# Sample attention of a hybrid decoder layer: steps for a pair of batches, scores of 64 rows by 32 columns

## The chip, the core and the metric

The kernel runs on one core of a Trainium2 chip. The core has five engines that run their own instruction streams: TensorE (PE: matmuls, with PEld for the weight loads that go beside them), VectorE (DVE), ScalarE (ACT), GpSimd (POOL) and SyncE (SP), which here issues the transfers (DMA) between the main memory and the on-chip memory. TensorE writes its results into banks of PSUM, from which VectorE and ScalarE read. The metric is the device time of one launch in microseconds.

## What the kernel computes

One layer for a prompt of 512 positions and for a sample group of 8 batches with 8 new positions each. The same normalised input goes through one combined projection `w_in` (2048 rows), then through sparse attention with three branches and a gated linear recurrence (RG-LRU), both of which are projected and merged. The sample group's attention is the part that the change touches:

```
q, kv..., g_nsa, g_att, x_rnn, g_rnn, gm_att, gm_rnn = _project(x, norm_g, w_in, ...)   # 16 heads of 64, 4 key heads
k_c, v_c = _compress(past_cmp, w_cmp, gain)           # 2048 past positions -> 64 compressed ones
o_cmp, imp = _cmp_branch(q, k_c, v_c, q_pos)          # softmax over them; importance of 32 blocks
sel_idx = _select_blocks(imp, q_pos)                  # the best 15 of 32 blocks of 64 positions
s = einsum('btgrd,btgkd->btgrk', q, k[selected]) * SCALE;  o_sel = softmax(s) @ v[selected]
s = einsum('btgrd,bkgd->btgrk', q, k[window 512]) * SCALE; o_win = softmax(s) @ v[window]
o_att = g_cmp * o_cmp + g_sel * o_sel + g_win * o_win
```

A batch has 8 positions x 4 query heads = 32 query rows for each of the 4 key heads, against 2048 past keys (in four blocks of 512, the unselected masked by a bias) and 512 window keys, a fifth block.

## The kernel before

The projections are the frame of the program. The weights go through in "slots": a slot is 24 matmuls of 128x128 by 288 columns (eight slices of weights, each three times: high part by high part, high by low, low by high), of which `L1710` to `L1712` are the three lines. The weights of a unit arrive by one transfer (`raw`, L226), ScalarE makes their high part (`whi`, L233) and VectorE the low part (`wlo`, L239), every second slot. All other work is put between the slots, and the order in which the Python code emits it is the order on each engine.

In the slots of the RG-LRU's two projections (168 to 231, 64 slots; 734 to 1026 us of the profile), the code emits, ahead of the slot's 24 matmuls: the weight split's high part, then the functions that were put on that slot by `at(slot, f)` (parts of the RG-LRU chunk: `split`, `decay`, `scan`), then the sample attention's next step (`sample_work`), then the low part and the next load of weights, then the read-out of finished projection banks, and last the functions put "behind" (the gate products `gate(0)`, `gate(1)` at L1242). An RG-LRU chunk has 8 slots. A gate product uses one bank of "s" and one of "t".

`sample_steps` writes out by hand what is done in which step: `put(t, order, f, x)` puts a function into step t, and within a step the smaller order goes first. Batch b has its scores of block n2 at step 8 + 5b + n2, and there are 52 steps, one in nearly every slot, so several batches are under way at once. For a block: `k_load` (L995, four transfers of 128 KB for four pages, three steps ahead), `v_load` (L1005), `k_scores` (L915, through `s_scores`), `k_max` on VectorE (L1019; L1024 and L1025 for the window: mask, maximum, copy out of the bank), `s_exp` on ScalarE (L1030), two steps later four transposes (L1035) and their copy (L1039), and one step after that the products with V (L1049) into the batch's output bank "o". `c_norm`, `c_root`, `c_keys`, `x_scores`, `x_exp`, `x_prob`, `x_sum`, `x_select` make the compressed branch and the choice of blocks (L892 to L957), `x_new`, `x_turn_`, `x_turned`, `x_out` the new keys (L963 to L986), and `s_factors`, `s_total`, `s_sum` (L1075, L1076), `s_fin` (L1080) and `s_put` (L1085) the end of a batch.

The score products of a batch are four matmuls, one for each key head:

```
for h in range(4):
    T.matmul(dst[h * 32:h * 32 + 32], x.q[:, h], k(h // 2), start=True, stop=True)
```

Each takes 128 rows of keys (two key heads stand one above the other, 64 rows each) by 32 columns of queries, whose other 64 rows are zero (`q_batch`). The four go to four column groups of the array and write the four quarters of one bank. In single precision each matmul is two passes, so it has two records in the trace.

PSUM has two banks each of "g" (projection), "s" and "t", and one of "o" and one of "m" (small products).

Of the kernel before, what the change touches and what calls it, by code (L numbers as in the profile page):

```python
# [16 lines left out]
KEPT = 3  # L17
# [96 lines left out]
def nsa_rglru_step(ctx, tc, a, o):  # L114
# [259 lines left out]
    gR = ar.tile([128, 3, DB], F, name="gR")  # L374
# [15 lines left out]
    def evac(kind, h, b):  # L390
# [9 lines left out]
        if name == "gn":  # L400
# [5 lines left out]
            if h == 1:  # L406
                def sigmoids():
                    V.tensor_mul(t[:48], t[:48], rstd[:48])
                    A.activation(t[:48], t[:48], AF.Tanh, scale=0.5)
                    V.tensor_scalar(t[:48], t[:48], 0.5, 0.5, op0=OP.mult, op1=OP.add)  # L410
                at(NORM + 2, sigmoids)

                def gates():
                    m = bank("m")
                    for i in range(4):
                        T.transpose(m[:, i * 48:i * 48 + 48], t[:48, i * 128:i * 128 + 128], ident[:48, :48])
                    V.tensor_copy(gT.rearrange("p i c -> p (i c)"), m[:, :192])
                at(NORM + 4, gates)

                def rows():  # L420
                    S.dma_start(gs_d, t[:48, 512:576])
                    for br in range(3):
                        S.dma_start(gR[:, br, :], gs_d[br * 16:br * 16 + 16, :].rearrange("g (t b) -> (g t) b", b=8))
                at(NORM + 4, rows)
# [415 lines left out]
    def q_batch(x):  # L840

        x.q = pp["s"].tile([128, 4, 32], F, tag="qb", name="qb", bufs=3)
        G.memset(x.q, 0.0)
        for c in range(2):
            for gl in range(2):
                me = slice(gl * 64, gl * 64 + 64)
                V.tensor_copy(x.q[me, c * 2 + gl].rearrange("p (r t) -> p r t", t=8), zs[me, c, :, x.b:64:8])

# [4 lines left out]
    for b, x in enumerate(batches):  # L853
        x.b = b
        x.P, x.T, x.V, x.K, x.cr = {}, {}, {}, {}, {}
# [21 lines left out]
    def c_reduce(x, n):  # L877
        if n == 0:
            x.kvx = pp["x"].tile([128, 4, 80], F, tag="skvx", name="skvx", bufs=3)
# [5 lines left out]
    def c_fetch(x):  # L885
        if x.b >= KEPT:
            x.kvx = pp["x"].tile([128, 4, 80], F, tag="skvx", name="skvx", bufs=3)
            S.dma_start(x.kvx[:, :, 8:72], kc_d[x.b])

    def c_square(x):  # L890
        x.sq = pp["s"].tile([128, 2, 64], F, tag="ssq", name="ssq", bufs=2)
        A.activation(x.sq, x.kvx[:, 0:2, 8:72], AF.Square)  # L892
        for c, new in ((0, kn), (2, vn)):
            for br in range(2):
                G.tensor_copy(x.kvx[:, c:c + 2, br * 72:br * 72 + 8], new[:, :, br, x.b:64:8])

    def c_norm(x):
        sq = x.sq
        m = bank("m")
        T.matmul(m[:, :128], C("bones"), sq.rearrange("p c n -> p (c n)"), start=True, stop=True)  # L900
        x.m = m

    def c_root(x):
        sq, m = x.sq, held_bank("m", x.m)
        V.tensor_scalar(sq.rearrange("p c n -> p (c n)"), m[:, :128], 1.0 / HD, EPS, op0=OP.mult, op1=OP.add)
        A.activation(sq, sq, AF.Sqrt)

    def c_keys(x):
        V.reciprocal(x.sq, x.sq)
        V.scalar_tensor_tensor(x.kvx[:, 0:2, 8:72], x.kvx[:, 0:2, 8:72], P("gk0"), x.sq, OP.mult, OP.mult)  # L910

    def s_scores(dst, x, k):

        for h in range(4):
            T.matmul(dst[h * 32:h * 32 + 32], x.q[:, h], k(h // 2), start=True, stop=True)  # L915

    def x_scores(x):

        x.m = bank("m")
        s_scores(x.m[:, :80], x, lambda c: x.kvx[:, c, :])  # L920
# [4 lines left out]
    def x_exp(x):  # L925
        m = held_bank("m", x.m)
        x.e = pp["s"].tile([128, 80], F, tag="se", name="se", bufs=3)
        x.sm = pp["s"].tile([128, 32], F, tag="ssm", name="ssm", bufs=4)
        sm = x.sm
        V.tensor_reduce(sm[:, CN:CN + 1], m[:, 8:72], axis=AX.X, op=OP.max, negate=True)  # L930
        V.tensor_add(x.e[:, 0:8], m[:, 0:8], C("snew"))
        V.tensor_add(x.e[:, 72:80], m[:, 72:80], C("snew"))
        A.activation(x.e[:, 8:72], m[:, 8:72], AF.Exp, bias=sm[:, CN:CN + 1], accum_out=sm[:, CS:CS + 1])

    def x_prob(x):
        sm = x.sm
        V.tensor_scalar_max(sm[:, CS:CS + 1], sm[:, CS:CS + 1], TINY)
        V.reciprocal(sm[:, CS:CS + 1], sm[:, CS:CS + 1])
        V.tensor_scalar_mul(x.e[:, 8:72], x.e[:, 8:72], sm[:, CS:CS + 1])

    def x_sum(x):
        x.m = bank("m")
        T.matmul(x.m[:, :64], C("rsum"), x.e[:, 8:72], start=True, stop=True)

    def x_select(x):
        m = held_bank("m", x.m)
        imp = pp["s"].tile([128, 32], F, tag="imp", name="imp", bufs=2)
        v8 = pp["s"].tile([128, 2, 8], F, tag="v8", name="v8", bufs=2)
        V.tensor_reduce(imp, m[:, :64].rearrange("p (n two) -> p n two", two=2), axis=AX.X, op=OP.add)
        V.memset(imp[:, 0:32:31], -2.0)  # L950
        V.max(v8[:, 0], imp)
        V.match_replace(imp, v8[:, 0], imp, -2.0)
        V.max(v8[:, 1], imp)
        V.memset(v8[:, 1, 5:8], -2.0)
        V.match_replace(imp, v8[:, 1], imp, -2.0)
        x.bias = pp["s"].tile([128, 32], F, tag="sbias", name="sbias", bufs=2)
        V.tensor_scalar(x.bias, imp, -1.5, NEG, op0=OP.is_gt, op1=OP.mult)  # L957

    def x_new(x):

        sm, e = x.sm, x.e
        for n, at_ in ((4, 0), (6, 72)):
            V.tensor_reduce(sm[:, NM + n:NM + n + 1], e[:, at_:at_ + 8], axis=AX.X, op=OP.max, negate=True)  # L963
        for n, at_ in ((4, 0), (6, 72)):
            A.activation(e[:, at_:at_ + 8], e[:, at_:at_ + 8], AF.Exp, bias=sm[:, NM + n:NM + n + 1],
                         accum_out=sm[:, SUM + n:SUM + n + 1])

    def x_turn_(x):
        t = x.tx = bank("t")
        T.transpose(t[:80, 0:128], x.e, ident)  # L970
        for c in range(2):
            T.transpose(t[:80, 128 + c * 128:256 + c * 128], x.kvx[:, 2 + c, :], ident)

    def x_turned(x):

        t = held_bank("t", x.tx)
        x.pt = pp["s"].tile([128, 640], F, tag="vx", name="vx", bufs=2)
        for n in range(3):
            A.activation(x.pt[:80, n * 128:n * 128 + 128], t[:80, :128], AF.Copy, scale=C("xm")[:80, n:n + 1])
        A.activation(x.pt[:80, 384:], t[:80, 128:384], AF.Copy)  # L980

    def x_out(x):
        ob = held_bank("o", x.o)
        for n, part in enumerate((4, 6, 7)):
            for h in range(4):
                T.matmul(ob[h * 32:h * 32 + 32, part * 64:part * 64 + 64], x.pt[:80, n * 128 + h * 32:n * 128 + h * 32 + 32],  # L986
                         x.pt[:80, 384 + h * 64:448 + h * 64], start=True, stop=True)

    def k_load(x, n2):

        t = pp["s"].tile([128, 1024], F, tag="kr", name="kr", bufs=4)
        if n2 < 4:
            x.K[n2] = t.rearrange("p (k c n) -> p k c n", k=4, c=2)
            for k in range(4):
                S.dma_start(t[:, k * 256:k * 256 + 256],  # L995
                            a["selk"][ds(page(x.b, 4 * n2 + k, "k"), 1)].rearrange("o p c f -> p (o c f)"))
        else:
            x.K[n2] = t.rearrange("p (c k n) -> p k c n", k=4, c=2)
            S.dma_start(t, a["wink"][x.b].rearrange("p c n -> p (c n)"))

    def v_load(x, n2):
        t = x.V[n2] = pp["s"].tile([128, 4, 256], F, tag="vr", name="vr", bufs=4)
        if n2 < 4:
            for k in range(4):
                S.dma_start(t[:, k], a["selv"][ds(page(x.b, 4 * n2 + k, "v"), 1)].rearrange("o p f -> p (o f)"))  # L1005
        else:
            S.dma_start(t, a["winv"][x.b])

    def k_scores(x, n2):
        x.s = bank("s")  # L1010
        t = x.K.pop(n2)
        s_scores(x.s.rearrange("p (k n) -> p k n", k=4), x, lambda c: t[:, :, c])

    def k_max(x, n2):

        s, sm = held_bank("s", x.s), x.sm
        p = x.P[n2] = pp["s"].tile([128, 512], F, tag="p", name="sp", bufs=4)
        if n2 < 4:
            V.tensor_tensor_reduce(p.rearrange("p (n k) -> p n k", k=64), s.rearrange("p (n k) -> p n k", k=64),  # L1019
                                   x.bias[:, n2 * 8:n2 * 8 + 8, None].to_broadcast([128, 8, 64]), -1.0, 3.0e38,  # L1020
                                   OP.add, OP.min, sm[:, NM + n2:NM + n2 + 1])
        else:
            to = sm[:, NM + 5:NM + 6]
            V.tensor_tensor_reduce(p[:, :8], s[:, :8], C("wm"), -1.0, 3.0e38, OP.add, OP.min, sm[:, CN:CN + 1])  # L1024
            V.tensor_tensor_reduce(p[:, 8:], s[:, 8:], C("zero").to_broadcast([128, 504]), -1.0, sm[:, CN:CN + 1],  # L1025
                                   OP.add, OP.min, to)

    def s_exp(x, n2):
        p, n = x.P[n2], n2 + n2 // 4
        A.activation(p, p, AF.Exp, bias=x.sm[:, NM + n:NM + n + 1], scale=-1.0, accum_out=x.sm[:, SUM + n:SUM + n + 1])  # L1030

    def s_turn(x, n2):
        t = x.t = bank("t")
        for k in range(4):
# [778 lines left out]
```

## Time and profile before

| what | value |
|---|---|
| median of 3 runs | 1663.26 us (1661.42 to 1664.68) |
| the profiled execution's own time | 1661.96 us |
| its span in the trace | 1660.2 us, 34348 instructions |
| TensorE busy | 1620.8 us (98% of the span) |
| VectorE, ScalarE, GpSimd busy | 1133.5 us (68%), 788.2 us (47%), 300.7 us (18%) |
| the chain that ended last | PE 72%, DVE 13%, ACT 9%, DMA 3%, issue 3% |
| score products (L915) in the chain | 2% of the span |

Busy is the time during which an engine had at least one instruction under way. The chain is followed back from the last instruction, at each step to what released it. The span begins a little after the launch and so is shorter than the time.

### The profile page before, as it was taken

The numbers are of one execution on the slowest core, as the hardware profiler recorded it, in microseconds if no ns is written. First come the engines' busy times: TensorE is split into PE (matmuls) and PEld (weight loads), VectorE is DVE, ScalarE is ACT, GpSimd is POOL, SyncE is SP. The second block draws the span as 40 slices with busy tenths as digits, with TensorE's granted clock in tenths as the row PEclk, the third lists the DMA queues.
The fourth block names the chain that finished last, engine by engine and source line by source line (L and its number), as shares of the span: only waits on it lengthen the run. The fifth ranks groups of instructions, "written<-read, shape, count | busy, mean of one in ns | idle before, by whom it ended". The sixth has DMA issues, their size and how long they took to land.

```text
span 1660.2 us, 34348 instructions
## 1 busy us (share of the span) xinstructions
PE 1620.8 (98%) x13309; PEld 1552.1 (93%) x13309; DVE 1133.5 (68%) x2259; ACT 788.2 (47%) x1449; POOL 300.7 (18%) x367
## 2 busy tenths in 40 slices
PE   9989999999999999999999999999998999999999
PEld 8989989998998999997878879999998999999999
DVE  7768778867876886566666766766665443358775
ACT  6353554555355454467776766444443222233332
POOL 0014443543444254400000000000000111110000
PEclk9999999999999999999999999999999999999999
DMA  6186634533533444437667673732337454456442
GB/s 229 62 292 236 198 105 122 176 108 100 183 122 114 135 151 144 139 122 233 211 209 239 221 227 98 231 133 107 123 127 256 149 165 160 142 198 225 135 154 74
DMA packets 132486, 272.18 MB, mean 164 GB/s; under 512 B 20321, under 2 KB 60386, under 8 KB 132066
## 3 DMA queue, kind: packets, MB, share of 16 engines
q1 hardware_dynamic: 132322, 269.98, 49.5%
q8 instruction: 105, 1.72, 0.4%
q14 instruction: 59, 0.48, 0.1%
HBM read 235.16 MB, written 43.15 MB: 168 GB/s over the span
## 4 chain that ended last, share of the span: by engine, by line
PE 72%; DVE 13%; ACT 9%; DMA 3%; issue 3%; SPq 1%; POOL 0%; ACTq 0%; DVEq 0%; POOLq 0%
PE g L1710 15%; PE g L1712 15%; PE g L1711 15%; DVE wlo L239 2%; PE g L1373 2%; PE g L1372 2%; PE g L1371 2%; ACT whi L233 2%; PE g L1471 2%; PE g L1473 2%; PE g L1472 2%; PE s L915 2%; PE t L748 1%; DVE pt L752 1%; ACT p L733 1%
## 5 line engine op out<-in xcount | busy, mean ns | idle before, releaser
L1710 PE MATMUL g<-xh,whi 128*128 128x288 f32 x1920 | 577.8, 301 | 0.1
L1712 PE MATMUL g<-xh,wlo 128*128 128x288 f32 x1920 | 567.5, 296 | 1.6 <-DVE wlo L239 1.6
L1711 PE MATMUL g<-xl,whi 128*128 128x288 f32 x1920 | 567.2, 295 | 0.0
L1710 PEld LDWEIGHTS g<-xh,whi 128*128 128x128 f32 x1920 | 362.5, 189 | 24.3 <-issue 18.3
L1711 PEld LDWEIGHTS g<-xl,whi 128*128 128x128 f32 x1920 | 362.5, 189 | 1.3
L1712 PEld LDWEIGHTS g<-xh,wlo 128*128 128x128 f32 x1920 | 361.8, 188 | 2.0 <-DVE wlo L239 2.0
L239 DVE TENSOR_TENSOR wlo<-raw,whi 128x1024 fp32r<-128x1024 f32 x164 | 221.4, 1350 | 33.4 <-ACT whi L233 32.1
L875 POOL TENSOR_TENSOR cr<-cr,wcs 128x512 f32<-128x512 f32 x128 | 182.6, 1431 | 164.1 <-DMA cr<-in_cmp 149.0
L233 ACT ACTIVATE whi<-raw 128x1024 fp32r<-128x1024 f32 x164 | 172.4, 1051 | 33.3 <-PE g L1711 24.2
L733 ACT ACTIVATE p<-p,sm,rq 128x128 f32<-128x128 f32 (+3 forms) x128 | 82.8, 648 | 154.4 <-DVE sm L730 154.2
L752 DVE TENSOR_TENSOR pt<-t,pt 128x512 fp32r<-128x512 f32 x96 | 66.1, 689 | 64.3 <-ACT pt L751 63.1
L741 POOL TENSOR_SCALAR p<-p,sm 128x128 f32<-128x128 f32 (+3 forms) x128 | 68.0, 544 | 208.3 <-DVE sm L738 88.0
L576 POOL TENSOR_TENSOR ur<-ur,tgi 128x288 f32<-128x288 f32 x32 | 25.7, 804 | 410.5 <-DVE tgi L575 338.6
L881 DVE TENSOR_REDUCE skvx<-cr 128x16 f32<-128x512 f32 x128 | 86.7, 678 | 0.4
L1710 PE MATMUL g<-hrh,whi 128*128 128x288 f32 x256 | 76.7, 299 | 6.5 <-ACT gm L532 4.2
L751 ACT ACTIVATE pt<-t 128x512 fp32r<-128x512 f32 x96 | 56.5, 592 | 55.0 <-PE t L748 54.3
L582 ACT ACTIVATE mh<-ur 128x288 fp32r<-128x288 f32 x32 | 14.2, 445 | 143.1 <-POOL ur L576 143.1
L1712 PE MATMUL g<-hrh,wlo 128*128 128x288 f32 x256 | 76.0, 297 | 0.0
L1711 PE MATMUL g<-hrl,whi 128*128 128x288 f32 x256 | 76.0, 297 | 0.0
L1712 PE MATMUL g<-oah,wlo 128*128 128x288 f32 x256 | 75.4, 295 | 0.0
L1711 PE MATMUL g<-oal,whi 128*128 128x288 f32 x256 | 75.3, 294 | 0.0
L1710 PE MATMUL g<-oah,whi 128*128 128x288 f32 x256 | 75.3, 294 | 0.0
(435 smaller groups left out, 3673.6 us busy)
## 6 DMA issues: line engine op xcount, KB each, us to landing
raw<-in_w_in SPq DMA_DIRECT2D x124, 512.0 KB, 3.6
cr<-in_cmp SPq DMA_DIRECT2D x128, 256.0 KB, 3.6
kr<-in_selk SPq DMA_DIRECT2D x128, 128.0 KB, 3.2
vr<-in_selv SPq DMA_DIRECT2D x128, 128.0 KB, 3.7
a<-in_w_in SPq DMA_DIRECT2D x28, 512.0 KB, 4.2
tgi<-tg SPq DMA_DIRECT2D x32, 288.0 KB, 4.4
yr<-in_w_out SPq DMA_DIRECT2D x18, 512.0 KB, 5.3
raw<-in_w_rnn SPq DMA_DIRECT2D x16, 512.0 KB, 4.5
```

What stands on the lines that cost most here:

```text
L233: A.activation(hi, raw[k], AF.Copy)
L239: V.tensor_sub(lo, raw.pop(k), hi.bitcast(F))
L733: A.activation(p[:, :n], p[:, :n], AF.Exp, bias=sm[:, 1, r - r0:r - r0 + 1], scale=rq[:, i, r:r + 1], accum_out=sm[:, 2, r - r0:r - r0 + 1])
L741: G.tensor_scalar(p[:, :n], p[:, :n], sm[:, 3, r - r0:r - r0 + 1], 1.0, op0=OP.mult, op1=OP.mult)
L751: A.activation(hi, t, AF.Copy)
L752: V.tensor_sub(lo, t, hi.bitcast(F))
L875: G.tensor_tensor(v, v, wcs[:, :, None, :].to_broadcast([128, 4, 4, 32]), op=OP.mult)
L881: V.tensor_reduce(x.kvx[:, :, 8 + n * 4:12 + n * 4], v, axis=AX.X, op=OP.add)
L915: T.matmul(dst[h * 32:h * 32 + 32], x.q[:, h], k(h // 2), start=True, stop=True)
L1710: T.matmul(gb[:, :HF], wh[:, k, :], r_h[:, hs], start=kk == 0, stop=False)
L1711: T.matmul(gb[:, :HF], wh[:, k, :], r_l[:, hs], start=False, stop=False)
L1712: T.matmul(gb[:, :HF], wl[:, k, :], r_h[:, hs], start=False, stop=last and k == 7)
```

## The change

The unit of the steps becomes a pair of batches. All 128 partitions of a row of work now hold two batches and two of the four key heads: unit u = 0 has the key heads in the upper 64 rows, u = 1 those in the lower 64. Scores are made by eight matmuls for a pair, each of 64 rows by 32 columns: four column groups (two batches by two key heads) in each half of the rows. The halves write two different "s" banks, one for each unit. The queries need no zeros (`q_pair`). `k_max`, `s_exp`, the transposes, their copy and the V products have the same sizes and the same number as before, two per step, one for each unit. The output banks of the units are "o" and "m"; what used "m" before now uses "t". The smaller functions (`x_prob`, `x_select`, `x_new`, `s_factors`, `s_total`) do both units in one instruction where they can; `s_put` makes 16 copies per pair in place of 4. The gates' factors come through `gB` (12 small transfers) and a copy on GpSimd.

Pair n has its scores at steps 5 + 6n to 9 + 6n, the window's block first, and there are 32 steps. `sample_work` spreads the steps evenly over the same 64 slots, so a step comes in every second slot, the one that does not split weights. Keys are loaded one step ahead, transposes are made one step after the scores, V products two.

```diff
     def s_scores(dst, x, k):
-        for h in range(4):
-            T.matmul(dst[h * 32:h * 32 + 32], x.q[:, h], k(h // 2), start=True, stop=True)
+        for n in range(2):
+            for c in range(2):
+                j = (n * 2 + c) * 32
+                for u in UNITS:
+                    T.matmul(dst[u][j:j + 32], x.q[ROWS[u], n, c * 32:c * 32 + 32], k(n, c)[ROWS[u]], start=True, stop=True)
...
     def k_scores(x, n2):
-        x.s = bank("s")
+        x.s = [bank("s") for _ in UNITS]
         t = x.K.pop(n2)
...
     def s_sum(x):
+        for u in UNITS:
+            ob = held_bank("om"[u], x.o[u]).rearrange("p (n d) -> p n d", d=64)
+            t = pp["s"].tile([128, 512], F, tag="p", name="to", bufs=4).rearrange("p (n d) -> p n d", d=64)
+            V.tensor_mul(t, ob, x.sm[:, u, FAC:FAC + 8, None].to_broadcast([128, 8, 64]))
+            V.tensor_reduce(x.t2[:, u], t.rearrange("p n d -> p d n"), axis=AX.X, op=OP.add)
...
     def s_put(x):
+        for n, y in enumerate(x.b):
+            for pr in range(2):
+                for u in UNITS:
+                    for c in range(2):
+                        V.tensor_copy(o6[pr * 64:pr * 64 + 64, c, u, :, :, y.b], m[:, u, n, c, :, pr, :])
...
-        for x in batches:
-            s = 8 + 5 * x.b
...
+        for x in pairs:
+            s = 4 + 6 * x.n
+            put(s, 4, x_scores, x)
...
+            put(s + 2, 5, x_sum, x)
+            put(s + 2, 7, x_select, x)
+            for k, n2 in enumerate((4, 0, 1, 2, 3)):
+                t = s + 1 + k
+                put(t - 1, 0, k_load, x, n2)
+                put(t + 1, 0, v_load, x, n2)
+                put(t, 4, k_scores, x, n2)
+                put(t, 8, k_max, x, n2)
+                put(t, 9, s_exp, x, n2)
+                put(t + 1, 1, s_turn, x, n2)
+                put(t + 1, 1.5, s_turned, x, n2)
+                put(t + 2, 2, s_out, x, n2)
...
+            put(s + 8, 3, x_out, x)
+            put(s + 8, 7, s_sum, x)
+            put(s + 9, 5, s_fin, x)
+            put(s + 9, 7, s_put, x)
```

The order of the instructions at two places. On TensorE, a step of the sample attention between two slots' matmuls, before (L1035 transposes, L1049 V products, L915 scores into "s" and, the last row but one, of the compressed keys into "m"):

```order
L1710 MATMUL g<-xh,whi 128x288
L1711 MATMUL g<-xl,whi 128x288
L1712 MATMUL g<-xh,wlo 128x288
L1035 MATMUL t<-cst,sp 128x128 x4
L1049 MATMUL o<-vr,spt 32x64 x16
L915 MATMUL s<-kr,qb 32x512 x4
L915 MATMUL m<-skvx,qb 32x80 x4
L1710 MATMUL g<-xh,whi 128x288
```

And after, at a step with a gate product of the RG-LRU behind it (L1078 transposes, L1095 V products into the banks "o" and "m", L941 scores, L1296 the gate product):

```order
L1764 MATMUL g<-xh,whi 128x288
L1765 MATMUL g<-xl,whi 128x288
L1766 MATMUL g<-xh,wlo 128x288
L1078 MATMUL t<-cst,sp 128x128 x8
L1095 MATMUL o<-vr,spt 32x64 x16
L1095 MATMUL m<-vr,spt 32x64 x16
L941 MATMUL s<-kr,qb 32x512 x8
L1296 MATMUL s<-xb,bdh 128x288
L1296 MATMUL s<-xb,bdl 128x288
L1296 MATMUL t<-xb,bdh 128x288
```

The transposes and V products of two units now stand in one step, the eight score matmuls write both banks "s", and the gate product, which takes the next "s" bank, stands right behind them.

On VectorE, the end of a chunk's scan (L1261 to L1277) with the end of one batch behind it, before (L1075 and L1076 are `s_sum`, L1019 is `k_max`, L930 belongs to `x_exp`):

```order
L1261 SCALAR_TENSOR_TENSOR hh<-aa,ti 128x576
L1262 COPY hout<-hh 128x1
L1263 COPY hout<-hh 128x8
L1277 TENSOR_TENSOR rg<-rg,hh 128x64
L1075 TENSOR_TENSOR to<-o,ssm 128x512
L1076 TENSOR_REDUCE t_10723<-to 128x64
L1019 ISA sp,ssm<-s,sbias 128x512
L1019 ISA ssm 128x1
L930 TENSOR_REDUCE ssm<-m 128x1
```

And after, at step 12 (L1315 to L1331 the scan, L1124 and L1125 `s_sum`, L975 to L980 the start of `x_select`; the two `k_max`, L1060, come eight rows further on):

```order
L1315 SCALAR_TENSOR_TENSOR hh<-aa,ti 128x576
L1316 COPY hout<-hh 128x1
L1317 COPY hout<-hh 128x8
L1331 TENSOR_TENSOR rg<-rg,hh 128x64
L1124 TENSOR_TENSOR to<-o,ssm 128x512
L1125 TENSOR_REDUCE t_10583<-to 128x64
L1124 TENSOR_TENSOR to<-m,ssm 128x512
L1125 TENSOR_REDUCE t_10583<-to 128x64
L975 TENSOR_REDUCE imp<-t 128x64
L976 MEMSET imp 128x2x2
L978 MAX v_10591<-imp 128x8
L979 MATCH_REPLACE imp<-v_10591,imp 128x32
```

Behind the scan there are now two units' sums and a pair's selection of blocks ahead of `k_max`, where one batch's sum stood before.

## Rows read from the trace of the kernel before

**Rows 1.** The busy time by stretch, here the sum of three stretches that make up 740 to 1010 us: busy us of each engine in 270 us, and their means per stretch (a mean of the three, not a share).

```profile
sum 270.00, PE 261.56 PEld 220.35 DVE 185.28 ACT 195.19 POOL 16.35; mean PE 87.19 PEld 73.45 DVE 61.76 ACT 65.06 POOL 5.45
```

**Rows 2.** TensorE's groups of instructions between 727 and 1030 us. Columns: line, engine, operation, output and inputs, tile, shape, count, then busy us and mean ns of one, then the idle time just before them and what ended it.

```profile
L1710 PE MATMUL g<-xh,whi 128*128 128x288 f32 x473 | 143.4, 303 | 0.0
...
L915 PE MATMUL s<-kr,qb 128*32 128x512 f32 x320 | 42.6, 604 | 0.0
...
L900 PE MATMUL m<-ssq,cst 128*128 128x128 f32 x16 | 3.3, 287 | 3.0 <-ACT ssq L892 3.0
...
L970 PE MATMUL t<-cst,se 128*80 128x128 f32 x8 | 2.3, 285 | 2.8 <-ACT ti L1245 2.6 <-ACT spt L1039 0.2
L1080 PE MATMUL m<-cst,t 128*64 128x128 f32 x7 | 2.0, 283 | 2.7 <-ACT se L933 2.7
```

**Rows 3.** TensorE's timeline at a cluster with a score block. Columns: start us, us from the first start to the last end, engine, line, operation, tiles, shape, records.

```profile
876.97 0.60 PE L1035 MATMUL t<-cst,sp 128*128 128x128 f32 x4
877.41 0.33 PE L943 MATMUL m<-se,cst 128*128 128x64 f32 x2
877.67 0.65 PE L1049 MATMUL o<-vr,spt 128*32 128x64 f32 x32
878.14 1.04 PE L915 MATMUL s<-kr,qb 128*32 128x512 f32 x8
879.11 0.40 PE L1710 MATMUL g<-xh,whi 128*128 128x288 f32 x1
```

**Rows 4.** The same view at a cluster of the last steps, which has no score block.

```profile
1013.02 0.60 PE L1035 MATMUL t<-cst,sp 128*128 128x128 f32 x4
1013.55 0.65 PE L1049 MATMUL o<-vr,spt 128*32 128x64 f32 x32
1014.13 0.40 PE L1710 MATMUL g<-xh,whi 128*128 128x288 f32 x1
1014.37 0.29 PE L1711 MATMUL g<-xl,whi 128*128 128x288 f32 x1
1014.50 0.29 PE L1712 MATMUL g<-xh,wlo 128*128 128x288 f32 x1
```

**Rows 5.** The same view at the longest wait of this stretch (in brackets: idle us before, and what ended it).

```profile
777.75 0.60 PE L1035 MATMUL t<-cst,sp 128*128 128x128 f32 x4
780.89 0.49 PE L900 MATMUL m<-ssq,cst 128*128 128x128 f32 x2 [2.54 <-ACT ssq L892]
...
781.78 1.77 PE L915 MATMUL s<-kr,qb 128*32 128x512 f32 x8
```

**Rows 6.** The busy time by stretch, just after that wait: busy us and instructions of PE, PEld, DVE, ACT and POOL, the granted clock as a share of full speed, the DMA engines' share and GB/s.

```profile
782.00:785.00 3.00, 3.00 (x14) 1.52 (x7) 2.96 (x9) 1.20 (x3) 2.29 (x8) 0.50 0.81 268
```

**Rows 7.** VectorE's groups of instructions between 740 and 1010 us, columns as in Rows 2.

```profile
L1019 DVE CUSTOM_DVE_ANT_1 sp<-s,sbias 128x512 f32<-128x512 f32 x32 | 21.9, 685 | 15.9 <-PE s L915 15.9
...
L1261 DVE TENSOR_TENSOR_SCAN hh<-aa,ti 128x576 f32<-128x576 f32 x7 | 9.5, 1358 | 0.2
L1263 DVE COPY hout<-hh 128x8 f32<-128x8 f32 x7 | 9.3, 1326 | 0.0
...
L1076 DVE TENSOR_REDUCE t<-to 128x64 f32<-128x512 f32 x7 | 7.5, 1078 | 0.2
...
L1255 DVE TENSOR_TENSOR ti<-ti,tr 128x576 f32<-128x576 f32 x7 | 5.3, 754 | 0.3 <-ACT tr L1250 0.3
L1025 DVE CUSTOM_DVE_ANT_0 sp<-s,cst,ssm 128x504 f32<-128x504 f32 x7 | 5.2, 743 | 0.2
...
L1075 DVE TENSOR_TENSOR to<-o,ssm 128x512 f32<-128x512 f32 x7 | 4.8, 686 | 2.8 <-PE o L1049 2.8
...
L1019 DVE DVE_READ_ACCUMULATOR2_ANT ssm<- 128x1 f32 x32 | 2.6, 83 | 0.0
```

**Rows 8.** The busy time by stretch, from the first to the last instruction of one batch's selection (L949 to L957, ten instructions on VectorE), columns as in Rows 6.

```profile
877.78:879.42 1.64, 1.64 (x42) 0.80 (x42) 1.33 (x10) 1.53 (x3) 0.14 (x1) 1.00 0.87 264
```

**Rows 9.** ScalarE's groups of instructions between 740 and 1010 us, columns as in Rows 2.

```profile
L1030 ACT ACTIVATE sp<-sp,ssm 128x512 f32<-128x512 f32 x39 | 28.0, 719 | 39.4 <-DVE ssm L1019 27.4 <-DVE ssm L1025 11.9
L233 ACT ACTIVATE whi<-raw 128x1024 fp32r<-128x1024 f32 x25 | 26.2, 1050 | 0.8 <-PE g L1711 0.6
...
L1250 ACT ACT_TABLE_LOAD x7 | 9.0, 1283 | 0.1
...
L1030 ACT ACTIVATION_READ_ACCUMULATOR sp<-sp,ssm 128x1 f32 x39 | 7.3, 187 | 0.0
...
L1249 ACT ACTIVATE tr<-tr,lc 128x576 f32<-128x576 f32 x7 | 6.1, 870 | 0.2
L1245 ACT ACTIVATE ti<-s,lc 64x288 f32<-64x288 f32 x12 | 6.0, 498 | 0.1
...
L1248 ACT ACTIVATE aa<-tr,lc 128x576 f32<-128x576 f32 x6 | 5.1, 852 | 0.0
...
L1250 ACT ACTIVATE tr<-tr 128x576 f32<-128x576 f32 x7 | 4.8, 686 | 0.1
```

**Rows 10.** SyncE's timeline: issues of transfers, from the first one's start to the last one's end.

```profile
871.09 1.88 SPq L1005 DMA_DIRECT2D vr<-in_selv  x4
873.22 2.70 SPq L995 DMA_DIRECT2D kr<-in_selk  x4
```

**Rows 11.** The waits of SyncE's queue between 734 and 1026 us: who waited, for what, us in total, times, the longest.

```profile
SPq L226 <- DVE wlo L239: 65.3, 14, 8.6
```

More of the change, by code (lines that the diff above doesn't have):

```diff
@@ L838, in q_sample @@
             at(now[0] + 1 + n, f)
[L840 to L847, printed above, removed]
     class Batch:
@@ L886, in c_fetch @@
         if x.b >= KEPT:
-            x.kvx = pp["x"].tile([128, 4, 80], F, tag="skvx", name="skvx", bufs=3)
+            x.kvx = pp["x"].tile([128, 4, 80], F, tag="skvx", name="skvx", bufs=4)
             S.dma_start(x.kvx[:, :, 8:72], kc_d[x.b])
-    def c_square(x):
[L891 to L895, printed above, removed]
+    class Pair:
+        pass
@@ new lines, in nsa_rglru_step, with q_pair @@
+    pairs = [Pair() for _ in range(DB // 2)]
+    for p, x in enumerate(pairs):
+        x.n, x.b = p, batches[2 * p:2 * p + 2]
+        x.K, x.V, x.P, x.T, x.t = {}, {}, {}, {}, {}
+    UNITS = range(2)
+    ROWS = slice(0, 64), slice(64, 128)
+    def q_pair(x):
+        x.q = pp["s"].tile([128, 2, 64], F, tag="qb", name="qb", bufs=2)
+        z = zs.rearrange("p c r t -> p (c r) t")
+        for n, y in enumerate(x.b):
+            V.tensor_copy(x.q[:, n].rearrange("p (r t) -> p r t", t=8), z[:, :, y.b:64:8])
@@ L897, in c_norm @@
+    def c_square(x):
+        x.sq = pp["s"].tile([128, 2, 2, 64], F, tag="ssq", name="ssq", bufs=1)
+        for n, y in enumerate(x.b):
+            A.activation(x.sq[:, n], y.kvx[:, 0:2, 8:72], AF.Square)
+            for c, new in ((0, kn), (2, vn)):
+                for br in range(2):
+                    G.tensor_copy(y.kvx[:, c:c + 2, br * 72:br * 72 + 8], new[:, :, br, y.b:64:8])
     def c_norm(x):
-        sq = x.sq
-        m = bank("m")
-        T.matmul(m[:, :128], C("bones"), sq.rearrange("p c n -> p (c n)"), start=True, stop=True)
@@ L945, in x_select @@
+        T.matmul(x.m[:, :128].rearrange("p (u n) -> p u n", u=2), C("rsum"), x.e[:, :, 8:72], start=True, stop=True)
     def x_select(x):
[L946 to L952, printed above, removed]
@@ L962, in x_new @@
         for n, at_ in ((4, 0), (6, 72)):
[L963 to L966, printed above, removed]
-    def x_turn_(x):
[L969 to L972, printed above, removed]
+            V.tensor_reduce(x.sm[:, :, NM + n:NM + n + 1], x.e[:, :, at_:at_ + 8], axis=AX.X, op=OP.max, negate=True)
@@ L982, in x_out @@
+        A.activation(x.pt[:80, 768:1024], t[0][:80, 256:512], AF.Copy)
+        A.activation(x.pt[:80, 1024:], t[1][:80, :256], AF.Copy)
     def x_out(x):
[L983 to L987, printed above, removed]
-    def k_load(x, n2):
-        t = pp["s"].tile([128, 1024], F, tag="kr", name="kr", bufs=4)
-        if n2 < 4:
-            x.K[n2] = t.rearrange("p (k c n) -> p k c n", k=4, c=2)
-            for k in range(4):
[L995 to L999, printed above, removed]
@@ L1028, in s_exp @@
[L1028 to L1034, printed above, removed]
-            T.transpose(t[:, k * 128:k * 128 + 128], x.P[n2][:, k * 128:k * 128 + 128], ident)
-    def s_turned(x, n2):
-        x.T[n2] = pp["s"].tile([128, 4, 128], F, tag="pt", name="spt", bufs=3)
-        A.activation(x.T[n2].rearrange("p k q -> p (k q)"), held_bank("t", x.t), AF.Copy)
@@ new lines, in v_load, with k_scores @@
+    def v_load(x, n2):
+        x.V[n2] = []
+        for n, y in enumerate(x.b):
+            t = pp["s"].tile([128, 4, 256], F, tag="vr", name="vr", bufs=4)
+            x.V[n2].append(t)
+            if n2 < 4:
+                for k in range(4):
+                    S.dma_start(t[:, k], a["selv"][ds(page(y.b, 4 * n2 + k, f"v{n}"), 1)].rearrange("o p f -> p (o f)"))
+            else:
+                S.dma_start(t, a["winv"][y.b])
+    def k_scores(x, n2):
+        x.s = [bank("s") for _ in UNITS]
+        t = x.K.pop(n2)
+        s_scores([b.rearrange("p (k n) -> p k n", k=4) for b in x.s], x, lambda n, c: t[n][:, :, c])
@@ new lines, in s_out @@
+    def s_out(x, n2):
+        if n2 == 4:
+            x.o = bank("o"), bank("m")
+        v, at_ = x.V.pop(n2), (n2 + n2 // 4) * 64
+        for u in UNITS:
+            ob, pt = held_bank("om"[u], x.o[u]), x.T.pop((n2, u))
+            for k in range(4):
+                for j in range(4):
+                    h = (j % 2 * 2 + u) * 64
+                    T.matmul(ob[j * 32:j * 32 + 32, at_:at_ + 64], pt[:, k, j * 32:j * 32 + 32], v[j // 2][:, k, h:h + 64],
+                             start=k == 0, stop=k == 3)
```

256 lines of the change are left out of this document (143 added, 113 removed).

## Prediction

> **What bounds the kernel now.** Read first the busy shares of the stretch that the change rewrites [rows 1]: from 740 to 1010 us TensorE is busy for 261.56 of 270 us, VectorE for 185 and ScalarE for 195. TensorE is the bound, so a microsecond of its work taken out counts in full, unless a wait grows in its place. Read next what TensorE does there [rows 2]: the projection's matmuls (L1710 and its two sisters) fill most of it; the sample attention is laid between them in clusters, and the score products (L915) are its largest part, 320 records, which is 160 matmuls of two passes, 40 blocks of four. The idle column names the only waits that TensorE shows there: 3.0, 2.8 and 2.7 us, together 8.5. Last read two clusters record by record, one with scores [rows 3] and one without [rows 4], since the price of a block is the difference between them, not the busy time of its records.
>
> **The score products.** In [rows 3] the eight records of a block take from 878.14 to the next projection matmul at 879.11, 0.97 us. Leaving narrow tiles for the projection costs 0.11 of it: the products with V (L1049) take 0.58 to the next start where the projection follows [rows 4], and 0.47 where scores follow, which have the same shape [rows 3]. A block so costs 0.86 us. Eight records of about 0.6 us each in 1.04 us are four streams side by side, each of two passes. The new block has eight streams, four columns by two halves of the rows, and serves two batches. No row of this trace has two halves of the rows at work together. Bounds: 0.86 us for the block (eight side by side) and 1.72 (one half after the other). I take 0.86: the halves use other rows of the array, other partitions of the operands and other banks, and the four column tiles, which share the rows, already run at once. Twenty blocks in place of forty then save 20 x 0.86 = 17.2 us.
>
> The Trainium skill says in "TensorE: Matmul & The Clock Gate", on reordering, that matmuls stay in program order. Two passes of one tile must follow each other, and in the compiled order they stand next to each other; strictly by that, the four matmuls of a block of today would take four times two passes, over 3 us, and the new one twice that. The 1.04 us of [rows 3] disagrees, so tiles do overtake; by the page's "TensorEngine Tiling (Array Packing)", Key Properties, tiles operate independently, which this row bears out for columns alone.
>
> **Clusters.** 52 clusters become 32, since a pair's step stands in every second slot. What a cluster costs beside its contents is in [rows 4]: four transposes take 0.53 us to the next start, of which 4 x 0.11 are theirs (0.60 for the four less 0.27 for one is three pitches); the change of shape is 0.10; the change back 0.11; and the first projection matmul runs 0.24 instead of 0.13, another 0.11. That is 0.32, so 20 fewer save 6.4 us. Against it, scores now have another shape than the V products ahead of them, which is one more change of shape in 24 clusters (20 steps and 4 score products of the compressed blocks), at the same 0.10 to 0.11: -2.5. Products made once per pair instead of once per batch (norm, importance, compressed scores) save about 1.5: their pieces are 0.1 to 0.3 each, as L943 shows with 0.26 less the change of 0.10 [rows 3], and half of the columns remain. Transposes, V products and the gate products of the RG-LRU keep their number. The sum of TensorE's work is 17.2 + 6.4 + 1.5 - 2.5 = 22.6 us less.
>
> **What it waits for now, and then.** The waits of today are 8.5 us, and a wait has an echo: after the 2.54 us at 780.89 [rows 5] the granted clock is 0.50 from 782 to 785 us [rows 6], 1.2 instead of 2.4 GHz, so half of 3 us is lost on top. With that, 10 us can vanish at most. New ones come from five places.
>
> First, the gate products (L1296, the bank "s") stand right behind the scores in six steps. A step now fills both of the two "s" banks, so the gate waits until k_max has read the first. That is 0.77 us of VectorE (L1019 and its read-out, 0.69 and 0.08 [rows 7]) and a hand-over, 0.9 us; before, one bank was left for it. In two of the six the block is the window's (two instructions, the longer 0.74 [rows 7], some 1.15 with the hand-over), in one VectorE makes 16 copies of s_put before k_max: they are small, and the ten small instructions of [rows 8] take 0.164 each with their gaps, so 16 are 2.6, and 3.5 with k_max. Sum: 3 x 0.9 + 2 x 1.15 + 3.5 = 8.5 us.
>
> Second, the step at which s_sum of one pair and x_select of the pair after it meet with k_max. There are three, t = 12, 18 and 24. VectorE needs for s_sum 2 x (0.69 + 1.08) = 3.5 [rows 7], for x_select 2.6 (1.64 us for ten instructions [rows 8], sixteen for a pair), for k_max 1.5; at t = 18 the next gate waits for the first k_max: 3.5 + 2.6 + 0.8 less the 1.2 us by which s_sum starts before the cluster ends and one slot of 3.3 between, 2.4 us.
>
> Third, at t = 12 and 24 the scan of an RG-LRU chunk stands ahead of these on VectorE: 0.75 + 1.36 + 1.33 [rows 7] and small ones, 4.3 us. It starts when ScalarE has finished that chunk's decay, and ScalarE has, from the cluster before: two s_exp with their read-outs 1.8, four tanh 2.0, a table load 1.28, a weight split 1.05, then 0.85 + 0.87 + 1.28 + 0.69 for the decay [rows 9], in all 9.8 us, beginning 0.9 after that cluster. The next cluster ends 6.4 + 1.4 + 3.6 = 11.4 us after it, so the scan starts only 0.7 us before its end, and the first probabilities are ready 4.3 + 3.5 + 2.6 + 0.8 + 0.9 - 0.7 = 11.4 us after it, where the next transposes want them 6.4 us after it. The wait is 5.0 and its echo 1.5: 6.5 us each, 13 for the two. A lower bound is 1 us each (scan already done).
>
> Fourth, norms and transposes of the new keys meeting ScalarE late, as L900 and L970 do today [rows 2]: 2.5 us in all, a third of today's. Fifth, keys that land late. Four loads of vr take 1.88 us and four of kr 2.70 on SyncE [rows 10]; a step now issues eight of each, 9.2 us at most, behind a load of weights that waits for VectorE's split (65.3 us in 14 waits today [rows 11]), and needs the last keys one step later, where today they were issued three steps ahead. From the split's end, 9.2 us and 3.2 to land are 12.4; the scores that use them come about 15 us after it. VectorE late by more than 3 us makes TensorE wait. Bounds 0 and 14 us (2 us in seven steps); I take 1.5, since the late steps are those already counted.
>
> The sum is 8.5 + 2.4 + 13 + 2.5 + 1.5 = 28 us against 10 now: 18 us come back. Net: 22.6 - 18 = 4.6 us less. Fewer table loads (33 instead of 43 in the program, 1.28 us each [rows 9]), four copies of q fewer per pair and the gate's route through gB lie on engines that are idle a quarter of the time, or before the stretch; they count nothing, and if the cover failed they would be in the chains above.
>
> The profiled execution took 1661.96 us, 1.3 under the median of the runs. 1661.96 - 4.6 = 1657.4 against its own time, 1658 to 1659 against the median. I say 1658.
>
> **Rivals.** (B) *The waits are absorbed.* For it: VectorE is idle a third of the time, and if the decay is done early, the third term falls to 2 and the fifth to 0; 28 becomes 15. Gain 17.6: 1646. Against it: the order of instructions on VectorE is fixed.
>
> (C) *The halves of the rows do not run together,* or only in part. Then the score block costs up to 1.72 and 17.2 us are not saved: 1658 + 17.2 = 1675; with half of it 1666.6. It decides for slower where a block takes over 1.26 us (4.6 + 3.3 = 7.9 us, over 20 blocks). For it: no row shows halves at work; against it: the column tiles do it.
>
> (D) *Slower, by SyncE.* The loads of keys go 16 to a step behind a weight load that waits for VectorE, and each wait of the third kind makes the next loads late as well. Beyond 9.4 us of waits for keys (1.5 taken and 7.9) the kernel is slower; at the bound of 14, 1670. For it: SyncE needs 9.2 of about 10.3 us of a step; against it: loads run ahead where the split is early.
>
> **How the numbers follow.** About 0.2%, 3.3 us, is what a measurement of this kernel can tell from no change. Forecast 0.45, with a range of its own from waits of 20 to 34 us, 1650 to 1664: faster 0.31, same 0.13, slower 0.01. B 0.12, all faster. D 0.23: same 0.09, slower 0.14. C 0.20: same 0.03, slower 0.17. Together faster 0.43, same 0.25, slower 0.32. The range takes in the forecast, B to its middle, D to just over its bound and the half of C: 1647 to 1672.
>
> **What would show it.** The score block's records in the profile after: 16 in about 1.0 us (right) or in 1.7 to 1.9 (C). In the list of waits: TensorE's gate products waiting for k_max, about 9 us; transposes waiting for s_exp behind the scan, about 10 us before echoes, at two steps; hardly any waits of scores for kr.  The prediction fails if the block is not 0.86, if the two long waits are absent, or if keys land late at more than two or three steps.

## The result: slower, and the profile after

The changed kernel takes 1686.01 us (median of 4 runs, 1680.69 to 1689.88) against 1663.72 us before: the ratio is 1.0134, with a 95% interval of 1.0103 to 1.0165. It is 22 us slower where 5 us less were forecast, and outside the range. Its own runs are 9 us apart; those of before 3.

The page of the profiled execution (1684.69 us): the span, and busy us and share of TensorE and VectorE.

```profile
span 1682.9 us, 34206 instructions
...
PE 1619.7 (96%) x13293; PEld 1559.1 (93%) x13293; DVE 1122.6 (67%) x2207; ACT 769.3 (46%) x1411; POOL 300.5 (18%) x361
```

TensorE has no more work than before (1619.7 us; 1620.8 before) and is idle for 63 us of the span, where it was idle for 39. The sample steps' stretch tells where. To compare the same work, it is taken here in both traces from one matmul of the projections to the matmul 56 slots later (of the 64 slots of the steps, which begin some 20 us earlier than 734 us; at its start the two traces are 0.1 us apart). The rows give the busy time of PE, PEld, DVE, ACT and POOL, the granted clock, DMA share and GB/s, first of after and then of before.

```profile
735.41:1052.07 316.66, 281.75 (x3464) 246.91 (x3463) 187.01 (x529) 190.18 (x394) 15.79 (x45) 0.96 0.60 192
```

```profile
735.34:1026.85 291.51, 283.07 (x3471) 241.09 (x3470) 196.61 (x584) 209.80 (x433) 16.35 (x56) 0.99 0.66 209
```

The 292 us have become 317. TensorE is idle for 35 us instead of 8. It is busy for about as long as before, but some of that at the lower clock, 1.2 in place of 2.4 GHz: the granted clock is 0.50 in seven places of the stretch, together 27 us, where it was 0.50 for the 3 us of [rows 6] alone. The sum of the seven, where PE is the busy time of TensorE:

```profile
sum 27.20, PE 25.32 PEld 21.22 DVE 10.74 ACT 14.69 POOL 0.00; mean PE 3.62 PEld 3.03 DVE 1.53 ACT 2.10 POOL 0.00
```

If half of that busy time is lost, the clock costs about 13 us, and 2 before (an estimate). The waits of TensorE in that stretch (engine, line, what it waited for: us in total, times, longest), which answer to the idle columns of [rows 2]:

```profile
PE s L1296 <- DVE ssm L1060: 9.1, 5, 4.1
PE s L941 <- DMA kr<-in_selk: 9.1, 7, 1.8
PE t L1078 <- ACT sp L1072: 8.1, 2, 4.1
PE t L969 <- ACT spt L1083: 4.4, 4, 1.4
PE s L1296 <- DVE ssm L1065: 2.3, 2, 1.2
PE s L941 <- DVE ssm L1113: 1.6, 1, 1.6
```

With one of 0.2 us that is left out they are 34.8 us, against 8.5. L941 are the scores, L1078 the transposes of the probabilities, L1296 the RG-LRU's gate products, L969 the importance sums. Of the three waits of [rows 2] none is left: what L900, L970 and L1080 did (now L922, L1000 and L1130) is not in the list.

The score block is what was hoped for. TensorE's timeline at the first one (start, us to the last end, records), to be read against 878.14 in [rows 3]:

```profile
748.72 1.09 PE L941 MATMUL s<-kr,qb 64*32 64x512 f32 x16
```

Sixteen records in 1.09 us, where eight took 1.04: the halves of the rows run side by side. But in eight of the twenty blocks the second batch's keys were not there, and the block fell into two. This one is step 14's:

```profile
855.14 1.06 PE L941 MATMUL s<-kr,qb 64*32 64x512 f32 x8 [1.45 <-DMA kr<-in_selk]
857.26 1.92 PE L941 MATMUL s<-kr,qb 64*32 64x512 f32 x8 [1.06 <-DMA kr<-in_selk]
```

TensorE waits 1.45 us for the first batch's kr, eight records run, it waits another 1.06, and the other eight take a block's time of their own, here 1.92 us at the low clock. From the first to the last record's start a whole block takes 0.50 to 0.66 us; the eight cut ones take 1.33 to 3.55, together 18.9, so 14.9 us more than eight whole ones at 0.50. Of these 14.9 us, 6 are idle time that the list of waits holds already.

### The profile page after: what moved, and what is told of

The parts are those of the page before. It is cut to its first block, busy times and chain, and to the rows that moved or that the text cites. A ratio compares the mean times of both kernels' runs of the same rounds, so it can differ in the third digit from the quotient of the medians.

```text
span 1682.9 us, 34206 instructions
## 1 busy us (share of the span) xinstructions
PE 1619.7 (96%) x13293; PEld 1559.1 (93%) x13293; DVE 1122.6 (67%) x2207; ACT 769.3 (46%) x1411; POOL 300.5 (18%) x361
## 4 chain that ended last, share of the span: by engine, by line
PE 43%; DVE 4%; ACT 3%; SPq 2%; DMA 2%; issue 1%; DVEq 0%
PE g L1764 8%; PE g L1766 8%; PE g L1765 8%; PE g L1425 2%; PE g L1426 2%; PE g L1427 2%; PE g L1527 2%; PE g L1526 2%; PE g L1525 2%; SPq L1045 1%; PE s L941 1%; PE t L1425 1%; PE t L1426 1%; PE t L1427 1%; ACT sp L1072 1%
## 5 line engine op out<-in xcount | busy, mean ns | idle before, releaser
L239 DVE TENSOR_TENSOR wlo<-raw,whi 128x1024 fp32r<-128x1024 f32 x164 | 221.5, 1350 | 51.3 <-ACT whi L233 50.3
```

The source lines that it names most:

```text
L239: V.tensor_sub(lo, raw.pop(k), hi.bitcast(F))
```

## The experiments

The changed kernel, 1686.0 us, is the base of e and g; before is 1663.5 us in these runs.

**Keys two steps ahead (e1).**

```diff
-                put(t - 1, 0, k_load, x, n2)
+                put(t - 2, 4.5, k_load, x, n2)
```

> The changed kernel with one edit: a pair's keys for step t are loaded in step t - 2, right behind that step's score products (whose buffers they take over), instead of at the head of step t - 1. Theory K (the keys land late, because SyncE issues them behind a load of weights that waits for VectorE): the waits of score products for kr (9.1 us in seven waits of TensorE, more where the block is cut in two) go, and with their echo in the clock some 15 to 20 us: about 1668. Rival V (the late steps are VectorE's, the keys only show it): the waits move to the transposes and gate products, within 4 us of the changed kernel's 1686. Rival Q (SyncE's queue or the transfers are full): waits for vr or for weights come in place of those for kr, again within 4 us.

Measured 1671.2 us (1667.7 to 1672.2), 1.0044 of before [1.0030, 1.0057]: 15 us less. No block is cut any more (0.50 to 0.90 us from first to last record), and what the list of waits has left is the rest:

```profile
PE t L1078 <- ACT sp L1072: 8.1, 2, 4.1
PE t L969 <- ACT spt L1083: 7.9, 4, 3.2
PE s L1296 <- DVE ssm L1060: 7.8, 5, 2.6
...
PE o L1095 <- DMA vr<-in_selv: 0.6, 1, 0.6
```

Theory K holds. The wait of L969 for a bank of "t" rises from 4.4 to 7.9 us, since it had been hidden at one step behind the keys: the longest, now 3.2 us, is at step 6, where the changed kernel waits for the second batch's keys first and then 0.34 us for this bank.

**Keys ahead of values on SyncE (g1).**

```diff
-                put(t - 1, 0, k_load, x, n2)
+                put(t - 1, -1, k_load, x, n2)
```

> The changed kernel with one edit: in a step SyncE issues the eight loads of keys ahead of the eight of values; both still one step ahead, and behind the load of weights. It asks which part of the lateness is the order on SyncE and which the distance. If it is the order (eight loads of values, 4 to 6.5 us of issue, stand between the weights and the keys): most of the 15 us by which eight score blocks are cut go, and V products wait for values in part: 6 to 12 us less than 1686. If it is the distance of one step behind a load of weights that waits for VectorE: the waits only change from kr to vr, and the time stays within 4 us of 1686.

Measured 1687.4 us (1685.8 to 1689.4). The wait changed its name, the sum of TensorE's waits hardly (34.2 us, 34.8 in the changed kernel):

```profile
PE o L1095 <- DMA vr<-in_selv: 8.1, 9, 2.4
...
PE s L941 <- DMA kr<-in_selk: 1.9, 1, 1.9
```

So it is not the order of the sixteen loads but that all sixteen come one step ahead, behind a load of weights. SyncE's timeline in the changed kernel, ahead of the cut block of step 14, shows the queue (issues, first start to last end):

```profile
837.33 0.55 SPq L1334 DMA_DIRECT2D hr<-rg  x1
843.51 0.35 SPq L226 DMA_DIRECT2D raw<-in_w_in  x1
845.07 5.80 SPq L1045 DMA_DIRECT2D vr<-in_selv  x8
851.12 4.01 SPq L1032 DMA_DIRECT2D kr<-in_selk  x8
```

No transfer is issued from 837.88 until VectorE's split of the weights at 842.26 (below) lets the next weights go at 843.51; then eight values, then eight keys until 855.13, for scores that TensorE reached at 853.7.

**The sum of the outputs behind the maximum (e2).**

```diff
-            put(s + 8, 7, s_sum, x)
+            put(s + 8, 9.5, s_sum, x)
```

> The changed kernel with one edit: s_sum (two products and two reductions, 3.5 us of VectorE) comes behind k_max and s_exp of its step, not ahead of x_select and k_max. Theory S (the three long waits, two of transposes for s_exp at 4.1 us and one of a gate product for k_max at 4.1, are VectorE's work ahead of k_max): each wait falls by up to 3.5 us, and the echoes of the two long ones too: 12 to 18 us less, about 1671. Rival: the output banks or the copies of s_put are late instead, and the wait moves one step on: within 4 us of 1686.

Measured 1674.9 us (1672.3 to 1676.1), 11 us less. Waits of TensorE:

```profile
PE s L941 <- DMA kr<-in_selk: 7.0, 6, 1.8
PE s L1296 <- DVE ssm L1060: 5.6, 5, 2.6
...
PE s L941 <- DMA kr<-in_wink: 2.4, 2, 1.5
...
PE t L1078 <- ACT sp L1072: 1.3, 2, 0.6
```

The two long waits of the transposes fall from 8.1 to 1.3 us, and the longest gate wait from 4.1 to 2.6; the keys are late as before (7.0 and 2.4 us, 9.3 before). Theory S holds, a little under its size. The changed kernel's own step 12 shows the chain that it cuts, TensorE first:

```profile
840.33 1.97 PE L1078 MATMUL t<-cst,sp 128*128 128x128 f32 x8 [4.05 <-ACT sp L1072]
842.23 1.08 PE L1095 MATMUL o<-vr,spt 128*32 128x64 f32 x32
```

And VectorE in the same step (start, us, line):

```profile
828.75 0.76 DVE L1309 TENSOR_TENSOR ti<-ti,tr 128x576 f32<-128x576 f32 x1 [1.00 <-ACT tr L1304]
...
832.51 0.27 DVE L1331 TENSOR_TENSOR rg<-rg,hh 128x64 f32<-128x64 f32 x1
832.70 0.68 DVE L1124 TENSOR_TENSOR to<-o,ssm 128x512 f32<-128x512 f32 x1
...
836.12 0.28 DVE L975 TENSOR_REDUCE imp<-t 128x64 f32<-128x128 f32 x1
...
838.50 0.20 DVE L985 TENSOR_SCALAR sbias<-imp 128x64 f32<-128x64 f32 x1
838.73 0.69 DVE L1060 CUSTOM_DVE_ANT_1 sp<-s,sbias 128x512 f32<-128x512 f32 x1
...
842.26 1.23 DVE L239 TENSOR_TENSOR wlo<-raw,whi 128x1024 fp32r<-128x1024 f32 x1 [2.22 <-ACT whi L233]
```

The scan's first product starts at 828.75, the two units' sums at 832.70, the selection at 836.12, k_max only at 838.73; s_exp follows on ScalarE, and the transposes at 840.33, 4.05 us late. The weight split (L239), which ScalarE's high part precedes, runs at 842.26, and with it SyncE's queue is late: one late step of VectorE also makes the keys of step 14 late, those of the cut block above. The edit does not cure that: in e2 the split stands behind the sums on VectorE, and the block of step 14 is still cut (3.33 us from first to last record). TensorE's clock falls as well (columns as above, the clock third from the end):

```profile
840.00:846.00 6.00, 5.67 (x97) 4.41 (x98) 1.86 (x9) 3.19 (x8) 0.00 (x0) 0.72 0.21 75
```

**Both gate products in the slot without scores (e3).**

```diff
-        at(now[0] + 4, lambda: gate(1), True)
+        at(now[0] + 3, lambda: gate(1), True)
```

> The changed kernel with one edit: the RG-LRU's second gate product of a chunk stands in the slot of the first, a slot without scores, not behind the scores of the next slot. Theory G (a gate product behind scores waits for k_max, because a step fills both banks): the waits of about 1.0 to 1.2 us behind six score blocks go, and the one of some 3 us behind the 16 copies: 8 to 10 us less, about 1677. Rival: the score products or the gate products of the one slot wait for ScalarE's four more tanh: nothing gained.

Measured 1675.6 us (1670.5 to 1682.4), 10 us less. The profiled execution is the longest of the four, but 6 us of that lie ahead of the stretch; the same 56 slots take 306.5 us in it instead of 316.7. All of TensorE's waits sum to 27.7 us instead of 34.8. Theory G holds. The one long wait of a gate product in its own slot, after step 18, is untouched by it; in the changed kernel it reads

```profile
911.08 0.37 PE L1296 MATMUL s<-xb,bdh 128*128 128x288 f32 x1 [4.11 <-DVE ssm L1060]
```

**Scores over all rows (e4).**

```diff
-        for n in range(2):
-            for c in range(2):
-                j = (n * 2 + c) * 32
-                for u in UNITS:
-                    T.matmul(dst[u][j:j + 32], x.q[ROWS[u], n, c * 32:c * 32 + 32], k(n, c)[ROWS[u]], start=True, stop=True)
+        for u in UNITS:
+            for n in range(2):
+                for c in range(2):
+                    j = (n * 2 + c) * 32
+                    T.matmul(dst[u][j:j + 32], x.q[:, n, u, c * 32:c * 32 + 32], k(n, c), start=True, stop=True)
...
```

Not shown is the part in `q_pair`, which makes the queries' tile twice as large, fills it with zeros on GpSimd and copies each batch's queries once per unit.

> The changed kernel with one part undone: queries padded with zeros again and each score product over all 128 rows, so that the eight matmuls of a pair's block are four side by side, twice, and no change of shape stands between V products and scores. Theory H (two halves of the rows run side by side and save 0.86 us a block): block 1.8 to 1.9 us; TensorE's work grows by 17.2 less 2.5 for the changes of shape, of which the blocks that wait for a second batch's keys (about eleven) hide up to 0.86 each: 5 to 15 us more, 1691 to 1701. Rival (the halves do not help, the block takes about the same): within 3 us of 1686.

Measured 1686.0 us (1684.8 to 1689.1): no difference, so the rival's number came. But not for its reason. The block takes 0.83 us longer:

```profile
748.31 1.92 PE L943 MATMUL s<-kr,qb 128*32 128x512 f32 x16
```

TensorE's work is some 14 us more (the block's 0.83 less 0.11 for the change of shape, twenty times), and its waits are 22.1 us instead of 34.8, 12.7 less:

```profile
PE t L1080 <- ACT sp L1074: 8.1, 2, 4.1
PE s L1298 <- DVE ssm L1062: 6.7, 3, 3.8
PE s L943 <- DMA kr<-in_selk: 3.6, 4, 1.3
...
PE t L971 <- ACT spt L1085: 1.1, 2, 0.6
```

The stretch's clock is also a little higher, 0.97 in place of 0.96. So the time that the halves save on TensorE was there and went into waits: in the changed kernel TensorE was not the engine that set the pace of these steps.

**The three edits together (f1), and with scores over all rows (f2).** f1 has the edits of e1, e2 and e3; f2 has that of e4 besides.

> The three edits that each gave time alone, together: keys loaded in step t - 2 behind that step's scores, s_sum behind k_max, both gate products of a chunk in the slot without scores. Alone they took 15, 11 and 10 us off the changed kernel's 1686. If they remove three separate kinds of wait, the sum holds: about 1650, and the kernel is faster than before (1663) by what its TensorE work is smaller. Rival (the waits share one cause, so that the first edit takes what the others would): 1660 to 1666.

> The same three edits, and scores over all 128 rows with padded queries (the edit that alone left the changed kernel at 1686). If the halves of the rows save TensorE 0.84 us a block and this was hidden because other waits set the pace, it must show here, where most of those waits are gone: 20 x 0.84 less 2.5 for the changes of shape, 14 us above the run with the three edits. Rival (the halves save nothing that counts, whatever the waits): within 3 us of it.

f1 takes 1655.5 us (1653.7 to 1656.8), 0.9948 of before [0.9930, 0.9966]: 30.5 us under the changed kernel, of the 36 that the three gave alone, and 8 us faster than before. Its waits of TensorE, and the same 56 slots with the clock:

```profile
PE t L969 <- ACT spt L1083: 5.4, 4, 2.3
PE t L1078 <- ACT ti L1299: 4.3, 4, 1.4
PE o L1095 <- DMA vr<-in_selv: 2.9, 8, 1.0
PE t L1004 <- ACT ti L1299: 2.1, 2, 1.3
PE t L1078 <- ACT sp L1072: 1.6, 2, 0.8
PE s L1296 <- DVE ssm L1060: 1.3, 2, 0.6
PE t L922 <- ACT spt L1083: 0.6, 1, 0.6
```

```profile
738.33:1022.69 284.36, 265.77 (x3465) 235.90 (x3463) 185.45 (x525) 188.96 (x393) 15.26 (x45) 1.00 0.66 213
```

The clock is back at 1.00. f2 takes 1660.5 us (1655.7 to 1661.8), 5 us more than f1, between the 14 of the one expectation and the 3 of the other. Its waits and the same 56 slots:

```profile
PE t L1080 <- ACT ti L1301: 4.5, 4, 1.4
PE t L1006 <- ACT ti L1301: 1.6, 2, 1.3
PE s L1298 <- DVE ssm L1062: 1.0, 2, 0.6
PE o L1097 <- DMA vr<-in_selv: 0.7, 3, 0.3
PE t L971 <- ACT spt L1085: 0.6, 1, 0.6
```

```profile
734.19:1022.96 288.77, 279.75 (x3464) 242.62 (x3463) 187.89 (x531) 189.96 (x393) 15.55 (x48) 1.00 0.66 210
```

They are 8.4 us in place of f1's 18.2. TensorE is busy for 14.0 us more, and 9.8 us fewer waits leave 4.4, by which this stretch is longer than that of f1. (As a whole the profiled execution of f2, 1655.7 us, is the shortest of its ten and no longer than that of f1, since it enters the stretch 4 us earlier.) So even with these edits two thirds of what the halves of the rows save is waited away again, above all for banks of "t" (L969) that ScalarE has not yet read.

**Scan one slot earlier (f3).** f1, with `decay` at `now + 4` and `scan` at `now + 5`.

> The same three edits, and the RG-LRU's decay and scan one slot earlier, which the gate products in one slot allow, so that the scan's 4.3 us of VectorE stand in a slot without scores. The long waits of transposes for s_exp at steps 12 and 24 should go to nothing: 2 to 4 us below the run with the three edits. Rival: ScalarE's decay now stands ahead of the copies of the transposes, and TensorE waits for those: 0 to 5 us above it.

Measured 1663.2 us (1660.3 to 1666.9), 8 us more than f1: outside both expectations. V products waited 5.8 us for values, where f1 has 2.9, and waits sum to 20.9 instead of 18.2. Most of the rest is the clock: it is 0.98 in the stretch, 0.50 for 10 us of it, where f1 has 1.00, so about 5 us by the same estimate. Which of the two edits brought these waits was not tested.

**Values two steps ahead as well (f5).** f1, with `v_load` at `put(t, 2.5, ...)`.

> The kernel with the three edits, and a pair's values loaded two steps ahead as well, right behind the V products whose buffers they take over. Its V products wait 2.9 us for vr in eight waits. If they are the last of the late loads, 2 to 4 us less than its 1655.5, about 1652.5. Rival: SyncE now waits for V products and for scores of TensorE in turn, and the loads of weights behind them come late: 1656 to 1662.

Measured 1654.5 us (1652.6 to 1657.1), 0.9944 of before [0.9927, 0.9960]: the waits for vr are gone from the list, the time is that of f1 within the spread of the runs, so neither the expected gain nor the rival's loss is shown.

## Why the prediction was wrong, by its own steps

*TensorE's work: right in its main term, too large in the others.* The score block was taken at 0.86 us. From its first start to the next projection matmul it takes 1.02 us in f1 (923.62 to 924.64), 0.91 without the 0.11 for leaving narrow tiles; e4 shows the 1.8 to 1.9 of the other bound. Rival C falls. The halves were to save 17.2 us less 2.5 for changes of shape, and f2 against f1 shows 14.0. But in all, TensorE is busy for 265.8 us in f1, where the clock is full throughout, and for 283.1 before, 281.4 without the estimated loss to the clock: 16 us less, for 22.6 forecast. Pairs without the halves (f2, 279.8) save 1.6 us, where clusters and products made once were to save 7.9. One reason stands in the timelines: the 52 clusters became 38 in the changed kernel and not 32, since gate products that stood in a cluster with a step now stand alone, nine times instead of five. By the forecast's 0.32 us each, 14 fewer are 4.5 us, not 6.4; the remainder stays open. The rule of the Trainium skill quoted there, that matmuls stay in program order ("TensorE: Matmul & The Clock Gate", in its Part 2 under "Step-by-step: what each phase is for"), is neither borne out nor refuted by these rows. Sixteen records of about 0.6 us stand in 1.09 us, eight starting within 0.05 us and eight some 0.45 us later, so tiles run together; which record is which pass no row tells. The prediction's "tiles do overtake" rests on an order of the passes that no row shows.

*Gates behind scores: right.* 8.5 us were forecast; the list has 11.4 for the gate products, 7.3 without the one of 4.1 at step 18, and e3 gave 10. *The step with scan, sums and selection: right in place and size.* Forecast was a wait of 5.0 us at steps 12 and 24; the two were 8.1 us together, 4 each. The chain runs as it was reckoned, scan, sums, selection, k_max, s_exp, and e2, which takes 3.5 us out of this chain, gave 11 with the gate at step 18. That gate was forecast at 2.4 us and took 4.1; with the keys early it is 2.6 at most.

*Late keys: wrong, and this is the step that failed.* They were priced at 1.5 us, "since the late steps are those already counted", with a bound of 14. They cost 15 by e1; that the cut blocks alone come to 14.9 too is in part chance, since e1 also changes other waits and the clock. The input that failed is a distance: the prediction had the 9.2 us of issue and the 12.4 to landing, and set against them 15 us from the split's end until the scores, which it had read from no row. At step 14 the rows above give 10.2 us (the split ends at 843.49, TensorE reaches the scores at 853.7), while the last key is issued 11.6 us after the split. Read in the same way, the eight cut blocks have 6.8 to 13.5 us, and the whole blocks of selected pages 11.7 to 17.9; where 16 loads stand behind the split and the trace tells of their landing, the last lands 12.4 to 15.6 us after it. Two more things were left out. The bounds were worked out as waits of TensorE for a load, but half of the keys being late does not delay a block, it cuts it: the batch that has its keys runs alone, and the other takes a block's time of its own behind it, so that the lateness also takes back what the pairing saved. And the lateness is not confined to the late steps: of the eight cut blocks (steps 6, 8, 9, 11, 14, 17, 23 and 26) only those of 14 and 26 come behind the long waits. The others too stand behind a weight split that comes once in two slots, with eight to sixteen loads between, 0.5 to 0.8 us each where they are pages. That is the sign of failure which the prediction named itself, keys late at more than two or three steps. Rival D had the mechanism and a chance of 0.23, but a price at its bound of 1670.

*Echo: under-sized.* 1.5 us was given to each of two waits, 3 us in all. By the estimate above the clock costs 13 us, 11 more than before, in seven places instead of one (behind one long wait, 840 to 846 us, the mean is 0.72).

*The importance sum's bank: left out.* L969 waits 4.4 us and has no term in the prediction: the 2.5 us of "norms and transposes" were for L900 and L970, whose waits are gone. The sum stood on bank "m" before and shares "t" with two transposes now. (Not all that used "m" went to "t": the scores of the compressed keys went to the two banks "s".)

Together, in the stretch: TensorE is idle 26 us more, and the clock costs 11 us more. The rest of its busy time is 12 us less, which is the 16 saved, less what the cut blocks' second halves cost. (That leaves 4 us for them; the blocks' own count leaves 9 that are not idle, some of it at the low clock. The two estimates are not reconciled.) These make the 25 us by which the stretch is longer. Behind it the two profiled executions come 2 us closer again, to the 23 us between their spans; those of the other runs differ there from before by 2 us less to 1 us more.

## What to carry to other kernels

When TensorE's work in a stretch is cut, price the chain behind it at the new pace: the same loads, copies and reductions must now come in less time and in larger bursts, and an engine that was 98% busy hid them. The distance at which a load is issued should be counted from the slowest thing ahead of it in its queue, not from the step that it stands in. A saving should be tested where it sets the pace: the score halves were worth nothing in the changed kernel and 5 us once three orders were changed.

## What was not expected of the hardware

A block of products over several tiles does not start as a whole: the first batch's matmuls stand first in the program, and with that batch's keys present 8 of 16 records ran and the rest followed 0.9 to 2.9 us later in a time of their own. With two halves of the rows, eight tiles streamed 512 columns in two passes in 1.09 us, and four tiles over all rows in 1.04, so no cost for the second half was seen beyond 0.05 us.
